# Convolution sums kept in PSUM, low parts of weights made on GpSimd, first tap on ScalarE

## The chip, the cores and the metric

One NeuronCore of a Trainium2 chip runs the whole kernel. The metric is the device time of one execution in microseconds (us). The engines are named as the profile names them: PE is TensorE (matmuls; PEld its weight loads), DVE is VectorE, ACT is ScalarE, POOL is GpSimd and SP is SyncE, which here only issues DMAs.

## The reference, cut to what matters

Two model blocks are computed for 512 latent tokens and 256 context tokens of width 1024. The first block has two layers; each layer projects the normalised input by one wide matrix and feeds a convolution module, a gated linear attention (GLA) with four heads that runs in both directions, and a softmax attention. The second block is not touched by the change. The convolution module is what the change is about:

```python
CONV_WIDTH = 31
def conv_module(val, glu, gate, dw_w, dw_b, ln_g, ln_b, w_o):
    u = val * jax.nn.sigmoid(glu)
    pad = CONV_WIDTH // 2
    u = lax.conv_general_dilated(u, dw_w[:, None, :], window_strides=(1,),
                                 padding=[(pad, pad)],
                                 dimension_numbers=('NWC', 'WIO', 'NWC'),
                                 feature_group_count=D_CONV) + dw_b
    u = jax.nn.silu(layer_norm(u, ln_g, ln_b)) * jax.nn.silu(gate)
    return u @ w_o
```

So each of the 512 channels is convolved over time with its own 31 weights. The GLA keeps a state per head, in chunks of 64 tokens: `S_t = diag(a_t) S_{t-1} + k_t^T v_t`, `o_t = q_t S_t`.

## The kernel before, in words

**Projections.** Activations lie transposed: channels on the 128 partitions, tokens along the free axis. Float32 precision is made from two fp32r parts: a matrix `w` is split into a high part `wh` and a low part `wl = w - wh`, the activations likewise into `hh` and `hl`. A projection of 1024 inputs onto 128 outputs loads one weight tile `wr` (128x1024) by DMA, ACT makes `wh` (line 283), DVE makes `wl` (line 284), and PE runs three matmuls per block of 128 inputs (`hh` by `wh`, `hl` by `wh`, `hh` by `wl`; all record line 315) into a PSUM tile `pp`. Three of the eight PSUM banks belong to `pp`, the other five in this stage to the pool `glaps`, whose tiles are called `pm`. ACT or DVE evacuates `pp`.

**The stage around the change.** In `_first_block`, for each layer, several generators are written into each other by `_weave`, and the tile scheduler then sets the order on each engine by the order of writing and by readiness. The first `_weave` joins on its main side `conv_in` (eight projections; ACT makes two 128x768 tiles `tf` of a pair, lines 791 and 794, and DVE multiplies them to the convolution input `u`, line 796), `conv_gate` (four projections, lines 818 to 820), `gla_in` (the low-rank projection, whose weights DVE splits in line 904, then queries and keys, lines 930 and 931, and values, line 917), and the first steps of the heads. Its other side is `conv_mix` and then `conv_norm`. The second `_weave` joins the four GLA heads with `merge`, the product of the convolution output and its merge gate.

**`conv_mix`.** For each of four chunks of 128 channels, DVE runs 31 taps over a row of 783 columns (512 latent tokens, 15 zeros, 256 context tokens; 512 in layer 1). The first tap (line 806) writes the chunk's slice of the SBUF tile `ca`, and each of the other thirty (line 809) multiplies a shifted `u` by a per-channel weight (in `sm`) and adds `ca`. The four slices are independent of one another, so the scheduler may mix two chunks. There are 2 x 4 x 30 = 240 taps of line 809.

**`conv_norm`.** It sums the chunks (lines 829, 832), takes mean and variance by matmuls (lines 620, 630), normalises, gates and splits the result into `bh` (ACT, line 867) and `bl` (DVE, line 871). The product with `w_conv_out` follows.

**A GLA head.** `gla_gate` has the gate matmuls (line 943), their evacuation by ACT (lines 944, 945), exponential and logarithm (946, 947, the latter with a table load), a sum on DVE (948), two scans (951, 953), the last columns (957, 958), the decay on ACT (960), products with keys and queries (962 to 973) and a transpose on PE (979). `gla_body` has the state contributions (PE, line 993), the chain of 22 state updates `SP` on DVE (line 1003), which read the contributions from PSUM, the attention pairs (PE, line 1014; DVE, line 1016), the output (lines 1024 and 1028) and its norm. Each of these matmul groups takes one `pm` bank and holds it until the engine that reads it is done.

The functions that the change touches, with the line numbers of the profile:

Of the kernel before, what the change touches and what calls it, by code (L numbers as in the profile page):

```python
# [9 lines left out]
F32 = mybir.dt.float32  # L10
# [4 lines left out]
AF = mybir.ActivationFunctionType  # L15
ALU = mybir.AluOpType
AX = mybir.AxisListType
PSUM = bass.MemoryType.PSUM

P = 128  # L20
# [6 lines left out]
TAPS = 31  # L27
# [230 lines left out]
class _K:  # L258
# [12 lines left out]
    def split(self, spec, spare=None):  # L271

        nk, nc_ = spec[3], spec[5]
        n = nk * nc_
        r = self.raw(spec)[:, :n]
        if spare is None:
            hi = self.wh.tile([P, 1024], F32R, tag="wh", name="wh")[:, :n]
            lo = self.wh.tile([P, 1024], F32R, tag="wl", name="wl")[:, :n]
        else:
            c = slice(TX + P * spare, TX + P * spare + n // KT)  # L280
            hi, lo = self.hh[:, :, c], self.hl[:, :, c]
            r = r.rearrange("p (k c) -> p k c", k=KT)
        self.nc.scalar.activation(hi, r, AF.Copy)  # L283
        self.nc.vector.tensor_tensor(out=lo, in0=r, in1=hi.bitcast(F32), op=ALU.subtract)  # L284
        return hi, lo

    @staticmethod
# [266 lines left out]
def _weave(main, fill, n_main, n_fill, drain=True):  # L554

    acc = 0.0
    for _ in main:
        acc += n_fill / n_main
        while acc >= 1.0:
            acc -= 1.0  # L560
            next(fill, None)
    if drain:
        for _ in fill:
            pass


def _chain(*gens):
    for g in gens:
        yield from g


def _first_block(K, ctx, resp):
    tc, nc, a = K.tc, K.nc, K.a
    V, S, G, T = nc.vector, nc.scalar, nc.gpsimd, nc.tensor
# [8 lines left out]
    def layer(l, res, t3p, ctx2, pend):  # L583
# [21 lines left out]
        def vec(name, i=0, p0=0, p1=P, half=False):  # L605
            c = _S1[name] + i - (h0 if half else g0)
            return (smh if half else sm)[p0:p1, c:c + 1]
# [172 lines left out]
        AL = TX + 15 + TC if need else TX  # L780
# [3 lines left out]
        ca = big.tile([P, 4, AL], F32, tag="A", name="ca")  # L784
# [14 lines left out]

        def conv_mix():  # L800
            for c in range(4):
                for t0 in range(0, TAPS, 4):
                    for t in range(t0, min(t0 + 4, TAPS)):
                        x, w = u[:, c, t:t + AL], vec("cw", c * TAPS + t)
                        if t == 0:
                            V.tensor_scalar(out=ca[:, c, :], in0=x, scalar1=w, scalar2=vec("dwb", c), op0=ALU.mult,
                                            op1=ALU.add)
                        else:
                            V.scalar_tensor_tensor(out=ca[:, c, :], in0=x, scalar=w, in1=ca[:, c, :], op0=ALU.mult,  # L809
                                                   op1=ALU.add)  # L810
                    yield

        def conv_gate(gt):
# [59 lines left out]
            yield  # L873


        with tc.tile_pool(name="gla", bufs=1) as gp, tc.tile_pool(name="glaps", bufs=8 - K.pp_banks, space=PSUM) as pm:
            masks = gp.tile([P, 2, P], U8, name="masks")
            mf = t3(256)
            nc.scalar.dma_start(out=mf.rearrange("p (a b) -> p a b", a=2), in_=a["masks"])
# [162 lines left out]
            AT = [gp.tile([P, 512], F32, name=f"at{d}") for d in range(2)]  # L1042
            for t_ in AT:
                G.memset(t_, 0.0)
            cin, cb = conv_in(), []
            next(cin)
            next(cin)
# [4 lines left out]
            def gla_():  # L1052

                yield from gla_gate(0)
                for hd in range(4):
# [7 lines left out]
            gla = gla_()  # L1063
            n_gla, n0 = (43, 3) if need else (27, 3)
            n_tap = 37 if need else 34
            _weave(_chain(cin, conv_gate(gt), gla_in(), itertools.islice(gla, n0)),
                   _chain(pend(t3, pm_) if pend else (), conv_mix(), conv_norm(gt, cb, pm_)), 15 + n0, n_tap)
            _weave(gla, merge(lambda: cb, "w_conv_out", 0, True), n_gla - n0, 28 if need else 16)


# [702 lines left out]
```

## Time and profile before

| quantity | value |
|---|---|
| runs | 2756.91, 2754.63, 2762.05 us; median 2756.91 |
| profiled execution | 2754.25 us, span 2752.4 us, mean granted PE clock 0.978 |
| PE busy | 2622.0 us (95% of the span), 15260 instructions |
| DVE busy | 1980.2 us (72%), 3689 instructions |
| ACT busy | 1087.8 us (40%), 1812 instructions |
| POOL busy | 27.4 us (1%), 93 instructions |
| chain that ended last, by engine | PE 79%, DVE 15%, ACT 3%, DMA 2%, issue 2% |
| in it, by line | PE line 315 64%, DVE taps (line 809) 4%, DVE low parts (284) 2%, DVE state updates (1003) 2% |

The span is the profiled execution from its first to its last instruction; the execution's own time is 1.85 us longer. Busy times are sums over the whole span, so they average over stages with different limits; the stages that matter here lie at 60 to 300 us (layer 0) and 940 to 1220 us (layer 1). The chain is followed back from the last instruction to what released each step.

### The profile page before, as it was taken

What the parts mean: (1) busy time and instruction counts of PE and PEld (TensorE: products, weight loads), DVE (VectorE), ACT (ScalarE), POOL (GpSimd) and SP (SyncE); (2) the same over time, 40 slices, a digit from 0 to 9 for tenths busy, and PEclk for the clock granted to TensorE, in tenths of its full rate; (3) what the DMA queues carried; (4) which work ended last, traced back from release to release, by engine and by line L of the source; (5) the groups of instructions that cost most, each with busy time, mean ns of one, the idle gap of its engine ahead of it and who ended that gap; (6) DMA issues with size and microseconds to landing.
All of it is one profiled execution on the core that took longest, in us unless ns stands there. A gap on an engine that the chain in (4) does not pass through costs nothing.

```text
span 2752.4 us, 38523 instructions
## 1 busy us (share of the span) xinstructions
PE 2622.0 (95%) x15260; PEld 2265.3 (82%) x15260; DVE 1980.2 (72%) x3689; ACT 1087.8 (40%) x1812; POOL 27.4 (1%) x93
## 2 busy tenths in 40 slices
PE   5998899999899999699999999999999999999998
PEld 3887778888788788578878888888888988888887
DVE  5998565677875599766888588775776786645655
ACT  3234423354532333534545345442333444422332
POOL 0000000000000000000000000000000000000000
PEclk9998999999999999899999999999999999999999
DMA  6210103112253232023134333344432332222322
GB/s 210 64 57 29 39 28 103 51 34 62 68 153 104 84 96 67 25 69 110 53 118 142 119 119 114 113 128 126 138 101 77 86 89 82 77 77 85 92 69 77
DMA packets 78116, 243.27 MB, mean 88 GB/s; under 512 B 9968, under 2 KB 16496, under 8 KB 77808
## 3 DMA queue, kind: packets, MB, share of 16 engines
q1 hardware_dynamic: 72448, 233.37, 27.7%
q10 hardware_dynamic: 5488, 7.44, 0.9%
q8 instruction: 120, 1.97, 0.3%
q14 instruction: 60, 0.49, 0.1%
HBM read 238.68 MB, written 2.10 MB: 87 GB/s over the span
## 4 chain that ended last, share of the span: by engine, by line
PE 79%; DVE 15%; ACT 3%; DMA 2%; issue 2%; ACTq 0%; DVEq 0%
PE pp L315 64%; PE pm L315 5%; DVE ca L809 4%; PE ov L1259 2%; DVE wl L284 2%; PE sc L1229 2%; DVE SP L1003 2%; PE tr L1249 2%; ACT wh L283 1%; PE pm L630 1%; PE pm L1028 1%; DMA m<-wpack 1%; PE pm L620 1%; PE pm L1652 1%; DVE t L953 1%
## 5 line engine op out<-in xcount | busy, mean ns | idle before, releaser
L315 PE MATMUL pp<-hh,wh 128*128 128x512 f32 (+1 forms) x2080 | 772.0, 373 | 31.9 <-ACT bk L931 13.2
L315 PE MATMUL pp<-hh,wl 128*128 128x512 f32 (+1 forms) x2080 | 767.5, 372 | 27.8 <-DVE wl L284 27.7
L315 PE MATMUL pp<-hl,wh 128*128 128x512 f32 (+1 forms) x2080 | 766.9, 371 | 1.0 <-DVE hl L467 0.9
L283 ACT ACTIVATE wh<-wr 128x1024 fp32r<-128x1024 f32 (+1 forms) x316 | 313.7, 994 | 701.3 <-PE pp L315 594.9
L284 DVE TENSOR_TENSOR wl<-wr,wh 128x1024 fp32r<-128x1024 f32 (+1 forms) x316 | 359.9, 1140 | 182.9 <-ACT wh L283 178.0
L315 PEld LDWEIGHTS pp<-hh,wh 128*128 128x128 f32 x2080 | 396.1, 191 | 99.3 <-ACT bk L931 13.8
L315 PEld LDWEIGHTS pp<-hh,wl 128*128 128x128 f32 x2080 | 395.6, 191 | 99.4 <-DVE wl L284 34.5
L315 PEld LDWEIGHTS pp<-hl,wh 128*128 128x128 f32 x2080 | 396.4, 191 | 65.7 <-DVE hl L467 3.5
L809 DVE SCALAR_TENSOR_TENSOR ca<-u,sm,ca 128x783 f32<-128x783 f32 (+1 forms) x240 | 201.6, 887 | 1.1
L315 PE MATMUL pp<-hh 128*128 128x256 f32 x544 | 155.3, 285 | 1.7 <-DVE vl L1559 1.7
L315 PE MATMUL pp<-hl,hh 128*128 128x256 f32 x544 | 155.1, 285 | 1.6 <-DVE hl L284 1.6
L315 PE MATMUL pp<-hh,hl 128*128 128x256 f32 x544 | 154.9, 285 | 0.0
L414 DVE CUSTOM_DVE_ANT_0 junk<-mw,cond,bmod 128x1024 bf16<-128x1024 f32 x104 | 132.7, 1276 | 2.8 <-DMA mw<-modw 2.5
L315 PE MATMUL pp<-wl,hh 128*128 128x256 f32 x448 | 127.7, 286 | 0.6 <-DVE wl L284 0.4
L315 PE MATMUL pp<-wh,hl 128*128 128x256 f32 x448 | 126.6, 284 | 0.0
L315 PE MATMUL pp<-wh,hh 128*128 128x256 f32 x448 | 125.8, 284 | 0.8 <-ACT tf L735 0.8
L315 PE MATMUL pp<-bh,wh 128*128 128x512 f32 (+1 forms) x288 | 105.3, 367 | 4.6 <-DVE merged L770 2.3
L315 PEld LDWEIGHTS pp<-hh 128*128 128x128 f32 x544 | 105.5, 194 | 4.0 <-issue 2.5
L315 PEld LDWEIGHTS pp<-hl,hh 128*128 128x128 f32 x544 | 105.5, 194 | 2.5 <-DVE hl L284 1.9
L315 PEld LDWEIGHTS pp<-hh,hl 128*128 128x128 f32 x544 | 105.4, 194 | 0.0
L315 PE MATMUL pp<-bl,wh 128*128 128x512 f32 (+1 forms) x288 | 103.3, 360 | 0.0
L315 PE MATMUL pp<-bh,wl 128*128 128x512 f32 (+1 forms) x288 | 103.0, 360 | 0.0
(371 smaller groups left out, 4833.2 us busy)
## 6 DMA issues: line engine op xcount, KB each, us to landing
wr<-wpack SPq DMA_DIRECT2D x308, 512.0 KB, 3.7
mw<-modw SPq DMA_DIRECT2D x80, 512.0 KB, 3.8
wr<-wpack SPq DMA_DIRECT2D x48, 256.0 KB, 2.6
m<-wpack SPq DMA_DIRECT2D x16, 512.0 KB, 8.4
cond<-cond ACTq DMA_DIRECT2D x5, 512.0 KB, 4.5
res<-xT SPq DMA_DIRECT2D x4, 512.0 KB, 4.8
tf<-xT SPq DMA_DIRECT2D x8, 256.0 KB, 2.8
out<-t SPq DMA_DIRECT2D x16, 128.0 KB, 1.8
```

Of the source, the lines that this page charges most:

```text
L283: self.nc.scalar.activation(hi, r, AF.Copy)
L284: self.nc.vector.tensor_tensor(out=lo, in0=r, in1=hi.bitcast(F32), op=ALU.subtract)
L315: mm(o, lhsT=lhs[a], rhs=r[b], start=first and p == 0, stop=last and p == 2)
L414: pin(V.tensor_tensor_reduce(out=junk, in0=w, in1=self.cond[:, v, :], scale=1.0, scalar=bias[:, j:j + 1], op0=ALU.mult, op1=ALU.add, accum ...
L620: T.matmul(p1[:, i:i + 1], lhsT=x[:, o:o + P], rhs=ones[:, 0:1], start=True, stop=True)
L630: T.matmul(p2[:, o:o + P], lhsT=r[:, i:i + 1].to_broadcast([P, P]), rhs=ident, start=True, stop=True)
L809: V.scalar_tensor_tensor(out=ca[:, c, :], in0=x, scalar=w, in1=ca[:, c, :], op0=ALU.mult, op1=ALU.add)
L953: V.tensor_tensor_scan(out=cum[64:128, ::-1], data0=reset[64:128, ::-1], data1=ls[64:128, ::-1], initial=0.0, op0=ALU.mult, op1=ALU.add)
L1003: V.scalar_tensor_tensor(out=SP[r, n_, :], in0=SP[r, c_, :], scalar=dec[r, c_:c_ + 1], in1=con[c_][r, :], op0=ALU.mult, op1=ALU.add)
L1229: T.matmul(sc[:, s - k0:e - k0], lhsT=qT[:, t * P:t * P + P], rhs=kT[pi][:, s:e], start=pi == 0, stop=pi == 1)
L1249: T.transpose(tr[:, jj * 256 + q * P:jj * 256 + q * P + P], pr[q][:, (j + jj) * P:(j + jj + 1) * P], ident)
L1259: T.matmul(ov, lhsT=vhl[:, kts[j0 + jj], g].rearrange("p a b -> p (a b)"), rhs=x_[:, jj * 256:jj * 256 + 256], start=j0 + jj + pi == 0, st ...
```

## The change

It has four parts. (1) The sum of a chunk is kept in a PSUM tile `acc` (called `pc`, 128x1024 float32, two banks, one buffer); each tap reads and writes it there, and the last tap writes the result to `ca`. (2) The first tap is an ACT activation with scale and bias into `acc`. (3) Between the start of `conv_in` and the end of the first `_weave` of each layer, the low part of a weight tile is made by POOL; the split of line 904 stays on DVE, and so do the low parts of the second `_weave`. (4) The pool `glaps` has three banks instead of five.

```diff
         self.nc.scalar.activation(hi, r, AF.Copy)
-        self.nc.vector.tensor_tensor(out=lo, in0=r, in1=hi.bitcast(F32), op=ALU.subtract)
+        E = self.nc.gpsimd if self.pool_lo else self.nc.vector
+        E.tensor_tensor(out=lo, in0=r, in1=hi.bitcast(F32), op=ALU.subtract)
         return hi, lo
...
             for c in range(4):
+                acc = pc.tile([P, 1024], F32, tag="pc", name="pc")[:, :AL]
                 for t0 in range(0, TAPS, 4):
                     for t in range(t0, min(t0 + 4, TAPS)):
                         x, w = u[:, c, t:t + AL], vec("cw", c * TAPS + t)
                         if t == 0:
-                            V.tensor_scalar(out=ca[:, c, :], in0=x, scalar1=w, scalar2=vec("dwb", c), op0=ALU.mult,
-                                            op1=ALU.add)
+                            S.activation(acc, x, AF.Identity, scale=w, bias=vec("dwb", c))
                         else:
-                            V.scalar_tensor_tensor(out=ca[:, c, :], in0=x, scalar=w, in1=ca[:, c, :], op0=ALU.mult,
-                                                   op1=ALU.add)
+                            V.scalar_tensor_tensor(out=acc if t < TAPS - 1 else ca[:, c, :], in0=x, scalar=w, in1=acc,
+                                                   op0=ALU.mult, op1=ALU.add)
                     yield
...
-        with tc.tile_pool(name="gla", bufs=1) as gp, tc.tile_pool(name="glaps", bufs=8 - K.pp_banks, space=PSUM) as pm:
+        with tc.tile_pool(name="gla", bufs=1) as gp, tc.tile_pool(name="glaps", bufs=3, space=PSUM) as pm, \
+                tc.tile_pool(name="convps", bufs=1, space=PSUM) as pc:
...
+            K.pool_lo = True
             cin, cb = conv_in(), []
...
+            K.pool_lo = False
             _weave(gla, merge(lambda: cb, "w_conv_out", 0, True), n_gla - n0, 28 if need else 16)
```

Lines shift: 284 becomes 285, 806 becomes 808, 809 becomes 810, the other lines of the stage move on by one (to 800) or two.

The order on the engines moves with it. On DVE, at the end of the first chunk of layer 0, stand before (`u` is the convolution input, `wl` a low part):

```order
L809 SCALAR_TENSOR_TENSOR ca<-u,sm,ca 128x783
L284 TENSOR_TENSOR wl<-wr,wh 128x1024
L809 SCALAR_TENSOR_TENSOR ca<-u,sm,ca 128x783
L806 TENSOR_SCALAR ca<-u,sm 128x783
L809 SCALAR_TENSOR_TENSOR ca<-u,sm,ca 128x783 x5
L284 TENSOR_TENSOR wl<-wr,wh 128x1024
L809 SCALAR_TENSOR_TENSOR ca<-u,sm,ca 128x783 x5
```

and now, with the last tap of the first chunk in the fifth row and the second chunk behind it:

```order
L810 SCALAR_TENSOR_TENSOR pc<-u,sm,pc 128x783 x12
L797 SCALAR_TENSOR_TENSOR u<-tf 128x512
L810 SCALAR_TENSOR_TENSOR pc<-u,sm,pc 128x783 x3
L797 SCALAR_TENSOR_TENSOR u<-tf 128x256
L810 SCALAR_TENSOR_TENSOR pc<-u,sm,pc 128x783
L810 SCALAR_TENSOR_TENSOR ca<-u,sm,pc 128x783
L810 SCALAR_TENSOR_TENSOR pc<-u,sm,pc 128x783 x8
```

The second chunk's first tap stood on DVE among taps of the first chunk; now the taps of one chunk stand in a row, with no low part between them.

On ACT, ahead of the second head of layer 0, stand before (`bk` are keys evacuated from `pp`, `dec` is the decay, which reads what DVE wrote to `last`):

```order
L283 ACTIVATE wh<-wr 128x1024
L960 ACT_TABLE_LOAD
L960 ACTIVATE dec<-last 128x12
L966 ACTIVATE t_2019<-t_2008 128x768
L964 ACTIVATE t_2016<-t_2016 128x768
L970 ACTIVATE t_2008<-t_2008 128x768
L930 ACTIVATE bk<-pp,sm 64x256
L931 ACTIVATE bk<-pp,sm 64x256
```

and now:

```order
L283 ACTIVATE wh<-wr 128x1024
L932 ACTIVATE bk<-pp,sm 64x256
L933 ACTIVATE bk<-pp,sm 64x256
L932 ACTIVATE bk<-pp,sm 64x256
L933 ACTIVATE bk<-pp,sm 64x256
L962 ACT_TABLE_LOAD
L962 ACTIVATE dec<-last 128x12
```

The four key evacuations of 256 columns moved ahead of the decay and its table load.

On PE, at the state contributions (`gv`, `kn`) and attention pairs (`bq`, `kin`) of the first head of layer 0, stand before:

```order
L315 MATMUL pp<-hl,wh 128x512
L993 MATMUL pm<-gv,kn 128x128 x4
L1014 MATMUL pm<-bq,kin 128x128 x4
L315 MATMUL pp<-hh,wl 128x512
L315 MATMUL pp<-hh,wh 128x512
```

and now:

```order
L995 MATMUL pm<-gv,kn 128x128 x4
L945 MATMUL pm<-lr,wup 128x512
L945 MATMUL pm<-lr,wup 128x256
L995 MATMUL pm<-gv,kn 128x128 x8
L1016 MATMUL pm<-bq,kin 128x128 x2
L316 MATMUL pp<-hh,wh 128x256
```

The four attention matmuls in one piece are split into twos, with projection matmuls between, and the gate matmuls of the next head (line 945 now) stand directly ahead of the second group of contributions.

## Rows read from the trace of the kernel before

**Rows 1.** Windows: us, then PE, PEld, DVE, ACT, POOL busy; clock; DMA.
```profile
80.00:100.00 20.00, 20.00 (x115) 17.62 (x114) 19.82 (x22) 4.62 (x7) 0.00 (x0) 1.00 0.23 68
...
260.00:280.00 20.00, 7.86 (x47) 6.66 (x45) 19.35 (x33) 13.97 (x20) 0.00 (x0) 0.71 0.01 1
```

**Rows 2.** Waits of PE, 60 to 290 us: total us, times, longest us.
```profile
PE pp L315 <- ACT bk L931: 13.2, 2, 8.1
PE pp L909 <- DVE wh L904: 4.7, 1, 4.7
```

**Rows 3.** Waits of PE, 940 to 1160 us, the largest.
```profile
PE pp L315 <- DVE wl L284: 10.4, 2, 8.9
```

**Rows 4.** Groups of DVE by form, 60 to 230 us: busy us, mean ns, idle.
```profile
L809 DVE SCALAR_TENSOR_TENSOR ca<-u,sm,ca 128x783 f32<-128x783 f32 x120 | 118.1, 1031 | 0.7
L284 DVE TENSOR_TENSOR wl<-wr,wh 128x1024 fp32r<-128x1024 f32 x17 | 20.7, 1220 | 3.0 <-ACT wh L283 3.0
...
L806 DVE TENSOR_SCALAR ca<-u,sm 128x783 f32<-128x783 f32 x4 | 2.7, 684 | 0.1
...
L796 DVE SCALAR_TENSOR_TENSOR u<-tf 128x256 f32<-128x256 f32 x4 | 1.7, 422 | 0.1
```

**Rows 5.** Timeline of DVE, both layers: start us, us together, instruction, count.
```profile
72.43 6.38 DVE L809 SCALAR_TENSOR_TENSOR ca<-u,sm,ca 128x783 f32<-128x783 f32 x6
...
96.39 1.22 DVE L284 TENSOR_TENSOR wl<-wr,wh 128x1024 fp32r<-128x1024 f32 x1
97.52 4.81 DVE L809 SCALAR_TENSOR_TENSOR ca<-u,sm,ca 128x783 f32<-128x783 f32 x5
...
969.61 3.89 DVE L809 SCALAR_TENSOR_TENSOR ca<-u,sm,ca 128x512 f32<-128x512 f32 x5
...
1056.49 4.06 DVE L809 SCALAR_TENSOR_TENSOR ca<-u,sm,ca 128x512 f32<-128x512 f32 x6
```

**Rows 6.** Groups of DVE by form, 940 to 1100 us.
```profile
L809 DVE SCALAR_TENSOR_TENSOR ca<-u,sm,ca 128x512 f32<-128x512 f32 x120 | 83.4, 744 | 0.4
...
L464 DVE SCALAR_TENSOR_TENSOR t<-res,gsc,nps 128x512 f32<-128x512 f32 x8 | 5.5, 738 | 0.0
```

**Rows 7.** Timeline of ACT, 258 to 285 us.
```profile
258.75 1.02 ACT L864 ACTIVATE cd<-cd,sm 128x768 f32<-128x768 f32 x1
...
276.18 0.21 ACT L960 ACTIVATE dec<-last 128x12 f32<-128x12 f32 x1 [0.96 <-DVE last L958]
...
279.10 0.47 ACT L930 ACTIVATE bk<-pp,sm 64x256 f32<-64x256 f32 x1
```

**Rows 8.** Timeline of PE, 255 to 285 us.
```profile
261.09 0.37 PE L1014 MATMUL pm<-bq,kin 64*128 64x128 f32 x1
...
281.07 0.80 PE L315 MATMUL pp<-hh,wh 128*128 128x512 f32 x1 [8.13 <-ACT bk L931]
```

**Rows 9.** Timeline of DVE, the twelve state updates of the first head.
```profile
267.24 4.49 DVE L1003 SCALAR_TENSOR_TENSOR SP<-SP,dec,pm 64x128 f32<-64x128 f32 x12
```

**Rows 10.** Timelines of DVE and of POOL, 940 to 941 us.
```profile
940.18 0.16 DVE L305 SCALAR_TENSOR_TENSOR t<-t,nv 128x4 f32<-128x4 f32 x1
940.61 1.09 DVE L891 TENSOR_SCALAR nbz<-sm 128x4 f32<-128x4 f32 x1 [0.27 <-PE pp L315]
...
940.64 0.74 POOL L882 MEMSET reset<- 128x768 bf16 x1 [888.35 <-PE pp L315]
```

**Rows 11.** Groups of POOL by form, whole run.
```profile
L1593 POOL TENSOR_SCALAR_AFFINE_SELECT t<-t 128x128 f32<-128x128 f32 x32 | 15.9, 498 | 89.8 <-ACT t L1590 89.8
...
L1044 POOL MEMSET at<- 128x512 f32 x4 | 2.0, 530 | 0.1
```

**Rows 12.** Timeline of DVE, state updates of a later head, layer 1.
```profile
1147.42 6.39 DVE L1003 SCALAR_TENSOR_TENSOR SP<-SP,dec,pm 64x128 f32<-64x128 f32 x17
```

**Rows 13.** Timelines of ACT and PE: a high part and its first matmul.
```profile
85.62 1.06 ACT L283 ACTIVATE wh<-wr 128x1024 fp32r<-128x1024 f32 x1 [2.00 <-PE pp L315]
...
93.88 0.40 PE L315 MATMUL pp<-hh,wh 128*128 128x512 f32 x1
```

## The prediction

> **What bounds the kernel now.** I read the busy time by stretches first. In layer 0's conv stage TensorE (PE) is busy 20.00 us of 20 while VectorE (DVE) is busy 19.82 of 20; in 260 to 280 us, at the hand-over to the GLA heads, PE does 7.86 of 20, with a granted clock of 0.71 [rows 1]. So through the conv taps both engines are full, and what DVE is late with is paid afterwards, in the stretch 220 to 285 us. The waits of PE name the holes: 4.7 us once for the low-rank weights that DVE splits in line 904, and 13.2 us in two pieces for the evacuation of keys by ScalarE (ACT), line 931 [rows 2]. In layer 1 the one large entry is 10.4 us for a low part of weights (line 284) that stands on DVE behind the scans [rows 3]. These 28 us are about all that the two stages have to give; the projections themselves are dense.
>
> **Low parts to GpSimd (POOL).** The 17 low parts of a layer cost DVE 1.220 us each [rows 4], and the next instruction starts 1.13 us after one (96.39 to 97.52) [rows 5]. Between the first and last tap of layer 0 DVE now has 14 of them, in the new order 2, because two of the merge come forward: 12 x 1.13 = -13.6 us of DVE. In layer 1 I count 14 fewer: -15.8 us. On POOL no such operation is in the trace. Its 128x512 memset takes 530 ns and its 128x128 select 498 ns [rows 11]: by the memset a 1024-wide one takes 1.0 us, by the select scaled with its columns up to 4.0. I take 2. It matters little, since what hides it is lead: the high part of one block is made at 85.62 + 1.06 us and its first matmul starts at 93.88 [rows 13], 7.2 us later, more than the upper end, and a projection comes only every 8 us. If that lead were gone, PE would wait by the difference, 0 to 3 us per projection.
>
> **First tap to ACT.** DVE loses four operations of 0.684 us [rows 4], about 0.6 us of issue each: -2.4 us, in layer 1 -1.8. ACT gains four; its nearest row, a scale-and-bias over 128x768, took 1.02 us [rows 7]. There is one accumulator. So the first tap of chunks 2 to 4 can start only when DVE has finished the chunk before, and the new DVE order puts the next taps directly behind. At each of three boundaries DVE stands still for about 1.02 us: +3 us, in layer 1 (two thirds as wide) +2.4. ACT waits in its queue meanwhile, with the evacuation of the next projection behind it. The banks of the projection's own pool cover that while it is under some 8 us.
>
> **Taps into PSUM.** This is the dearest unknown. Six taps of one chunk in a row took 6.38 us, (6.38 - 1.03) / 5 = 1.07 us from tap to tap; five that change between chunks took 4.81, (4.81 - 1.03) / 4 = 0.945 [rows 5]. The tap itself lasts 1.031 us [rows 4]. The difference is the wait for one's own result. Before, the scheduler mixes two chunks, and I count 18 neighbouring pairs of the same chunk in layer 0; with one accumulator 94 are neighbours. With spacings as in SBUF that is 76 x 0.125 = +9.5 us. In layer 1 the same two spacings are (3.89 - 0.75) / 4 = 0.785 and (4.06 - 0.75) / 5 = 0.66 [rows 5], 83 more pairs: +10.2 us. What writing PSUM costs no row shows. Reading it costs nothing: with one operand there, line 464 takes 738 ns, the tap of the same 512 columns all in SBUF 744 [rows 6]. I take 1.07 for the new spacing, nearest to that row. My bounds are 0.945, as if the wait vanished, and 1.20, as if the write took once more the same 0.125. The Trainium skill, "Perfetto Trace Analysis", section "Optimizing Scalar/DVE Operations", speaks against this edit: it charges a DVE instruction about 125 ns of access on PSUM against 60 on SBUF, which by an estimate from that page would add 0.065 us to each of 240 taps, 15.6 us of DVE. The rows on reading do not agree with it; no run here shows writing.
>
> **POOL against DVE.** A small DVE instruction that takes 0.16 us took 1.09 beside a 0.74 us memset on POOL [rows 10]: the two engines can block each other. By the Trainium skill, "SBUF — State Buffer", section "Who interferes with whom", a DVE instruction with two SBUF inputs contends with a POOL instruction that reads SBUF, one with a single SBUF input does not; so the taps would run free and the old form would not have. That no run here shows. I charge the operations other than taps: eight gate products (0.42 us for the 256-wide form, [rows 4]) and four merges come some 0.5 us after the high part is made, just when POOL works. With 1 to 2 us of standstill for three or four of them: +4.5 us in layer 0, +3 in layer 1. The lower bound is 0.
>
> DVE's sum to the last tap is -13.6 - 2.4 + 3 + 9.5 + 4.5 = +1.0 us in layer 0 and -15.8 - 1.8 + 2.4 + 10.2 + 3 = -2.0 in layer 1. **The freed DVE time is nearly all spent again.**
>
> **What PE gets.** Line 904 now stands behind 62 taps on DVE instead of 74 and behind no low part, over 12 us earlier, so its 4.7 us [rows 2] go. The 13.2 us [rows 2] go as well. The second stretch starts at 281.07 behind a 8.13 us wait [rows 8]: the key evacuations (279.10) stood on ACT behind the decay (276.18), which waits for DVE [rows 7]. In the new ACT order they stand ahead of it. But a new wait takes that place. GLA has three banks instead of five, and the first attention pair (261.09 now, [rows 8]) needs a bank that the chain of twelve state updates frees: it starts at 267.24 and lasts 4.49 us [rows 9], so to 271.7, a wait of about 10 us in place of 13.2. Layer 0 up to the first head: -4.7 - 3.2 + 1.0 = -6.9. Each of the three later heads waits for banks; by the state updates of a head (6.39 us for 17, 0.375 each [rows 12]) a bank comes three or so updates late: +1.1 us each, +3.3. Layer 0: -3.6 us. Layer 1: the late low part stands one step (about 1.5 us) earlier on DVE, conv ends 2 us earlier but PE is nearly full there (take -1), and three heads give back 1.1 each: -1.5 - 1 + 3.3 = +0.8. Nothing else in the program changes.
>
> **Sum.** -3.6 + 0.8 = -2.8 us against the profiled execution's 2754.25: 2751.5. That execution lies 2.66 us below the median of the runs shown, 2756.91; I put the forecast at **2752**. Some 0.3% (8.3 us, to 2748.6 or 2765.2) is what a measurement here can tell from no change.
>
> **Rivals.**
> 1. *Writing PSUM hides the chain* (spacing 0.945 in layer 0, 0.66 in layer 1). Conv ends 9.5 and 10 us earlier, and with little contention 14 and 13 us. Then the heads start earlier and PE's holes [rows 1 to 3] close: by at most 10 us in layer 0 and 8 in layer 1 beyond the sum, 2752 - 18 = 2734; half of it is 2743. For it: DVE is full there [rows 1], so each freed microsecond counts. Against: the wait for a result exists wherever the result lies.
> 2. *Slower: writing PSUM lengthens it.* Place: the 94 pairs of each layer. Each 0.01 us costs 0.94 us per layer; from 1.15 on, conv ends 7.5 us later in each layer, and as the norm, the merge and the heads hang on it, PE waits for nearly all: 1.15 gives 2752 + 15 = 2767, the bound of 1.20 gives 2776. It decides from about 1.145.
> 3. *Three banks starve the heads.* If each head waited for its whole chain (6.4 us [rows 12]) less the 1.1 counted, three heads in layer 1 alone lose 16 us: 2768. Against: the new PE order puts projections between the pairs.
> 4. *POOL blocks the taps*, 2 us of standstill for each of 34 low parts, not for some small operations alone: +68 - 7.5 = 60 us of DVE that PE waits for, some 2810. For it: [rows 10]; against: the operations of that row are others.
> 5. *No effect*: PE is the bound wherever the taps run, DVE's time is free. 2754 to 2757, inside my forecast.
>
> **Chances.** Forecast with rival 5: 0.45 (own range 2745 to 2762, of which 0.09 under 2748.6). Rival 1: 0.26, rival 2: 0.13, rival 3: 0.08, rival 4: 0.08. Faster by over 0.3%: 0.26 + 0.09 = 0.35; slower: 0.13 + 0.08 + 0.08 = 0.29; the rest 0.36. The range 2735 to 2773 leaves out rival 4 (0.08), the far half of rival 2 (0.06) and the far end of rival 1 (0.06).
>
> **What would show it.** Right: taps of 128x783 in PSUM 1.07 us apart; three DVE holes of about 1 us ahead of the second, third and fourth chunk, released by line 808; the 4.7 us wait gone; PE waiting some 10 us for a bank ahead of the first attention pair, where the wait for line 931 stood; POOL's low parts 1 to 3 us with no PE wait on them. Wrong: a spacing under 1.0 or over 1.14; taps of 2 us and more beside POOL; PE waits of over 3 us per head in the later heads.

## The result, and the profile after

The changed kernel takes 2779.01 us (median of 4 runs, 2777.62 to 2780.0) against 2757.05 us (4 runs, 2754.63 to 2762.05) of the kernel before on the same chip: a ratio of 1.0078, 95% interval 1.0066 to 1.009. It is 22 us slower. The forecast was 2752, the range ended at 2773.

The page of the changed kernel: the chain that ended last by line, and of the costliest groups the one of POOL (busy us, mean ns, idle before, releaser):

```profile
PE pp L316 66%; PE pm L316 5%; PE ov L1263 2%; PE sc L1233 2%; PE tr L1253 2%; DVE SP L1005 1%; DVE wl L285 1%; POOL wl L285 1%; PE pm L631 1%; PE pm L1030 1%; DMA m<-wpack 1%; ACT wh L283 1%; DMA wr<-wpack 1%; PE pm L1656 1%; PE pm L621 0%
...
L285 POOL TENSOR_TENSOR wl<-wr,wh 128x1024 fp32r<-128x1024 f32 x34 | 81.4, 2398 | 933.9 <-DVE nv L449 744.1
```

A low part takes POOL 2.40 us (the forecast took 2). The taps, 4% of the chain before, are no longer among its lines: most of the chain is PE's, 82% where it had 79%.

The groups of DVE by form, 60 to 230 us, answer to [rows 4]. Two of them, the values `gv` and the products `merged`, are not among those rows; before, they were:

```profile
L917 DVE TENSOR_TENSOR gv<-pp,t 128x512 f32<-128x512 f32 x6 | 4.1, 685 | 0.0
L820 DVE SCALAR_TENSOR_TENSOR merged<-tf 128x768 f32<-128x768 f32 x4 | 3.8, 955 | 0.0
```

and now:

```profile
L810 DVE SCALAR_TENSOR_TENSOR pc<-u,sm,pc 128x783 f32<-128x783 f32 x116 | 120.3, 1037 | 7.7 <-ACT pc L808 4.4
L797 DVE SCALAR_TENSOR_TENSOR u<-tf 128x256 f32<-128x256 f32 x4 | 5.4, 1360 | 5.0 <-ACT tf L795 5.0
L821 DVE SCALAR_TENSOR_TENSOR merged<-tf 128x768 f32<-128x768 f32 x4 | 4.5, 1137 | 0.0
...
L919 DVE TENSOR_TENSOR gv<-pp,t 128x512 f32<-128x512 f32 x6 | 4.1, 690 | 4.3 <-PE pp L316 4.3
```

and its timeline to [rows 5]:

```profile
72.23 11.78 DVE L810 SCALAR_TENSOR_TENSOR pc<-u,sm,pc 128x783 f32<-128x783 f32 x11 [1.14 <-ACT pc L808]
...
108.23 8.55 DVE L810 SCALAR_TENSOR_TENSOR pc<-u,sm,pc 128x783 f32<-128x783 f32 x8 [1.08 <-ACT pc L808]
```

Taps in PSUM come (11.78 - 1.03) / 10 = 1.075 us apart, and the hole at a chunk boundary is 1.08 us.

The waits of PE, 60 to 300 us, answer to [rows 2]:

```profile
PE pm L945 <- DVE SP L1005: 7.2, 1, 7.2
PE pp L316 <- ACT bk L933: 5.9, 2, 3.8
PE pp L316 <- POOL wl L285: 3.2, 4, 1.5
```

**Where the 22 us are.** The same instruction can be followed through both traces. The four splits of the convolution output in layer 1 (first row of each pair) and the third of the four splits of the heads' output `go` there (second row) are on DVE, before:

```profile
1116.01 2.48 DVE L871 TENSOR_TENSOR bl<-merged,bh 128x512 fp32r<-128x512 f32 x4
...
1294.66 0.68 DVE L745 TENSOR_TENSOR bl<-go,bh 128x512 fp32r<-128x512 f32 x1
```

and after:

```profile
1126.06 2.48 DVE L872 TENSOR_TENSOR bl<-merged,bh 128x512 fp32r<-128x512 f32 x4
...
1317.18 0.68 DVE L746 TENSOR_TENSOR bl<-go,bh 128x512 fp32r<-128x512 f32 x1
```

The first come 10.05 us later, the second 22.52. Read in the same way at five places, by the ends of the instructions, the kernels of this study stand against the kernel before as follows (one profiled execution each, us; A is the first sum of the chunks in layer 0, B the first split of `go` behind layer 0's heads, C the second convolution input of layer 1, D and E the two rows above):

| kernel | A | B | C | D | E | time, median |
|---|---|---|---|---|---|---|
| changed | +4.5 | +3.5 | +10.6 | +10.0 | +22.5 | 2779.0 |
| e1: three banks | -2.2 | +3.6 | +2.3 | +2.3 | +16.1 | 2771.1 |
| e2: GpSimd alone | +24.6 | +23.0 | +32.6 | +61.5 | +72.6 | 2826.4 |
| e3: PSUM sums, no GpSimd | +3.7 | +13.9 | +12.6 | +32.6 | +41.9 | 2795.9 |
| e4: banks given back | +6.2 | +1.6 | +9.3 | +8.9 | +20.3 | 2767.0 |
| e5: late GpSimd | +4.8 | +3.9 | +4.7 | +5.7 | +19.6 | 2775.4 |
| e6: e4 and e5 | +5.3 | +0.3 | +1.3 | +3.8 | +16.6 | 2774.6 |
| e7: e6, two sums | +3.6 | +1.5 | +2.6 | +2.7 | +6.6 | 2759.6 |
| e8: four banks | -0.7 | -1.1 | -3.0 | -3.0 | +7.4 | 2764.9 |
| e9: before, GpSimd in the heads | +1.5 | -1.4 | -2.4 | +10.3 | +35.3 | 2783.7 |
| e10: e9, first tap on ScalarE | +1.6 | -7.2 | -8.7 | -3.2 | +5.4 | 2760.6 |
| e11: before, first tap on ScalarE | -1.4 | -2.8 | -4.9 | -3.3 | +0.7 | 2751.1 |
| e12: e7, GpSimd in the heads | +4.4 | +0.3 | +0.5 | +8.3 | +22.5 | 2778.9 |
| e13: changed, filler | +4.2 | +3.2 | +10.5 | +9.9 | +12.1 | 2769.3 |
| e14: e11, filler | -2.6 | -4.1 | -6.2 | -4.6 | +0.9 | 2756.6 |
| e15: e7, filler | +5.8 | +0.5 | +1.7 | +1.9 | +5.1 | 2757.6 |

So the changed kernel loses 3.5 us in layer 0, some 7 at the start of layer 1 (B to C), nothing in its conv stage (C to D) and 12.5 in its heads (D to E). A single execution scatters by some microseconds: the profiled one of e13 took 2763.8 us and that of e8 2758.9, both some 6 us below their medians, those of e4 (2772.8) and e9 (2789.7) some 6 us above. The verdicts below rest on the medians, the places on the traces.

**The start of layer 1.** The norm of the layer's input is a chain of small DVE instructions and then splits (`hl`). DVE of the changed kernel:

```profile
941.12 3.39 DVE L302 TENSOR_SCALAR g<-g 128x4 int32<-128x4 int32 x1
...
945.92 2.21 DVE L305 TENSOR_TENSOR t<-y 128x4 f32<-128x4 f32 x1
...
968.82 4.67 DVE L468 SCALAR_TENSOR_TENSOR hl<-t,mod,hh 128x256 fp32r<-128x256 f32 x4
```

beside POOL:

```profile
941.00 2.40 POOL L285 TENSOR_TENSOR wl<-wr,wh 128x1024 fp32r<-128x1024 f32 x1 [744.10 <-DVE nv L449]
943.35 0.74 POOL L884 MEMSET reset<- 128x768 bf16 x1
...
945.78 2.34 POOL L285 TENSOR_TENSOR wl<-wr,wh 128x1024 fp32r<-128x1024 f32 x1
...
967.52 4.89 POOL L285 TENSOR_TENSOR wl<-wr,wh 128x1024 fp32r<-128x1024 f32 x2 [19.41 <-ACT wh L283]
```

Instructions of 0.16 to 0.17 us last 3.39 and 2.21 us. The second ends with POOL's low part (948.1 us); the first outlasts one (943.4) and ends at 944.5, among short memsets of POOL. Four splits, 0.42 us apart when nothing holds them, take 4.67 us together.

### The profile page after: what moved, and what is told of

It reads as the page before. It is cut to its first block, busy times and chain, and to the rows that moved or that the text cites. A ratio compares the mean times of both kernels' runs of the same rounds, so it can differ in the third digit from the quotient of the medians.

```text
span 2775.9 us, 38521 instructions
## 1 busy us (share of the span) xinstructions
PE 2641.7 (95%) x15260; PEld 2279.1 (82%) x15260; DVE 1972.0 (71%) x3647; ACT 1094.3 (39%) x1820; POOL 108.0 (4%) x127
## 4 chain that ended last, share of the span: by engine, by line
PE 82%; DVE 9%; issue 3%; ACT 3%; DMA 2%; POOL 1%; SPq 0%; ACTq 0%; POOLq 0%; DVEq 0%
PE pp L316 66%; PE pm L316 5%; PE ov L1263 2%; PE sc L1233 2%; PE tr L1253 2%; DVE SP L1005 1%; DVE wl L285 1%; POOL wl L285 1%; PE pm L631 1%; PE pm L1030 1%; DMA m<-wpack 1%; ACT wh L283 1%; DMA wr<-wpack 1%; PE pm L1656 1%; PE pm L621 0%
## 5 line engine op out<-in xcount | busy, mean ns | idle before, releaser
L285 DVE TENSOR_TENSOR wl<-wr,wh 128x1024 fp32r<-128x1024 f32 (+1 forms) x282 | 318.8, 1131 | 171.9 <-ACT wh L283 164.7
L810 DVE SCALAR_TENSOR_TENSOR pc<-u,sm,pc 128x783 f32<-128x783 f32 (+1 forms) x232 | 207.8, 896 | 13.1 <-ACT pc L808 6.3
L285 POOL TENSOR_TENSOR wl<-wr,wh 128x1024 fp32r<-128x1024 f32 x34 | 81.4, 2398 | 933.9 <-DVE nv L449 744.1
```

Of the source, the lines that this page charges most:

```text
L285: E.tensor_tensor(out=lo, in0=r, in1=hi.bitcast(F32), op=ALU.subtract)
L810: V.scalar_tensor_tensor(out=acc if t < TAPS - 1 else ca[:, c, :], in0=x, scalar=w, in1=acc, op0=ALU.mult, op1=ALU.add)
```

## The experiments

The runs of the kernel before that go with them have medians of 2754.5 us (e1 to e4), 2756.3 (e5 to e8), 2755.8 (e9 to e12) and 2756.8 (e13 to e15); for the changed kernel it was 2757.1. So two times of different groups can be 2 to 3 us nearer or farther than they look, and the ratios are the better measure there. "Lower parts" in the edits is line 284 (285 after the change).

**e1, three banks alone.** Edit to the kernel before:

```diff
-tc.tile_pool(name="glaps", bufs=8 - K.pp_banks, space=PSUM) as pm:
+tc.tile_pool(name="glaps", bufs=3, space=PSUM) as pm:
```

> The kernel before with three banks for GLA instead of five, nothing else. Theory A (the banks cost most of the loss): the four heads of layer 1, from the low part of the convolution output (1118.5 us before) to the last gated output, lose about 12 us as in the changed kernel, and layer 0 some 3; 2757 + 12 to 15, so 2769 to 2772. Rival B (the loss in the heads comes from the order that the other parts bring, not from the banks): within 3 us of 2757.

Measured: 2771.14 us, ratio 1.0057 (1.0042 to 1.0072). Theory A holds: up to D it is 2 us behind, at E 16. The state updates of a head show how the banks do it. Before, the 22 of the last head run in one piece on DVE (start, us together, count, idle before and its releaser):

```profile
1212.56 8.29 DVE L1003 SCALAR_TENSOR_TENSOR SP<-SP,dec,pm 64x128 f32<-64x128 f32 x22
```

With three banks the contributions they read are written in pieces, as banks come free, and DVE waits for PE:

```profile
1221.43 0.34 DVE L1003 SCALAR_TENSOR_TENSOR SP<-SP,dec,pm 64x128 f32<-64x128 f32 x1 [0.40 <-PE pm L993]
...
1224.12 2.62 DVE L1003 SCALAR_TENSOR_TENSOR SP<-SP,dec,pm 64x128 f32<-64x128 f32 x7 [1.69 <-PE pm L993]
...
1228.08 4.89 DVE L1003 SCALAR_TENSOR_TENSOR SP<-SP,dec,pm 64x128 f32<-64x128 f32 x13 [0.37 <-PE pm L993]
```

The chain takes 11.5 us (1221.43 to 1232.97) instead of 8.3, 3.2 more in this head. That accounts for a part of the 13.8 us between D and E; PE's own waits for state updates are short there (1110 to 1320 us: total, times, longest):

```profile
PE pm L1014 <- DVE SP L1003: 2.5, 4, 0.8
```

**e2, GpSimd alone**, with sums in SBUF and five banks. Edit to the kernel before:

```diff
-        self.nc.vector.tensor_tensor(out=lo, in0=r, in1=hi.bitcast(F32), op=ALU.subtract)
+        E = self.nc.gpsimd if self.pool_lo else self.nc.vector
+        E.tensor_tensor(out=lo, in0=r, in1=hi.bitcast(F32), op=ALU.subtract)
...
+            K.pool_lo = True
             cin, cb = conv_in(), []
```

> The kernel before with only the low parts on GpSimd in the conv stage; sums stay in SBUF, five banks. Taps then have two SBUF inputs. Theory A (GpSimd and a VectorE instruction with two SBUF inputs block each other): each of 34 low parts of about 2.4 us stops VectorE for up to 2.4 us, minus 28 x 1.13 us that VectorE saves: conv ends 10 to 20 us later per layer, 2757 + 20 to 40. Rival B (only particular instructions are blocked): taps keep 0.945 and 1.07 us spacing and VectorE gains 14 us per layer; 2740 to 2757.

Measured: 2826.36 us, ratio 1.0265 (1.0239 to 1.0291). Theory A holds, with more than it allowed: +24.6 us at A. By form, 60 to 240 us:

```profile
L810 DVE SCALAR_TENSOR_TENSOR ca<-u,sm,ca 128x783 f32<-128x783 f32 x120 | 141.9, 1231 | 1.0
L807 DVE TENSOR_SCALAR ca<-u,sm 128x783 f32<-128x783 f32 x4 | 6.8, 1702 | 0.1
```

A tap with both operands in SBUF costs 1.231 us in the mean instead of 1.031 [rows 4], so 120 x 0.2 = 24 us; the tap with its sum in PSUM, beside the same work of POOL, costs 1.037. That is the difference that the Trainium skill, "SBUF — State Buffer", section "Who interferes with whom", makes between two SBUF inputs and one, and here the runs show it. The first tap (line 807) has one SBUF input beside its scalars and was held all the same, 1.702 us instead of 0.684; the section excepts instructions that enter a two-port mode and names `tensor_scalar` among those that can.

That the 24 us of the taps equal A (+24.6) is a coincidence: the 14 low parts that left DVE give back 16 us up to A, and longer first taps (4 us), longer products `u` (2) and 10 us more of standing still take them again. In layer 1, between C and D, DVE stands still for 30 us instead of 4, for 16 of them waiting for the values' projections (line 918); theory A's sum has no such term, and why these projections are late was not followed.

**e3, sums in PSUM without GpSimd.** Edit to the changed kernel:

```diff
-            K.pool_lo = True
```

> The changed kernel with all low parts on VectorE again: sums in PSUM, first tap on ScalarE, three banks. Theory A (GpSimd's share of the loss is the 7 us at the start of layer 1, where it blocks the norm and the splits): that start is as before (u of the first chunk at about 963 us plus the shift of layer 0), but VectorE carries 12 to 14 low parts more in each conv stage, so conv ends 12 us later in layer 0 and PE waits: about 2785. Rival B (low parts on GpSimd only cost, because VectorE's time is free): 2770 or less.

Measured: 2795.89 us, ratio 1.0145 (1.0129 to 1.016). Neither number was right: GpSimd is worth 17 us to the changed kernel (2795.9 against 2779.0; 19 when each is set against its own runs of before), not 6. The place that theory A named holds: from B to C this kernel loses nothing (+13.9, +12.6) where both kernels with GpSimd there lose 7 and 10. Against e1, which has the same three banks, the sum in PSUM with ScalarE's first tap costs 2795.9 - 2771.1 = 24.8 us as long as VectorE makes all low parts. What VectorE or PE waits for in these 24.8 us was not followed.

**e4, banks given back** to GLA once the first weave is written. Edit to the changed kernel:

```diff
             K.pool_lo = False
+            late.close()
+            more.append(late.enter_context(tc.tile_pool(name="glaps2", bufs=2, space=PSUM)))
```

> The changed kernel, but the two banks of the sum go back to GLA when the first weave of the layer has been written (heads 2 to 4 have five banks again). Theory A (banks cost the 12 us in layer 1's heads): most of it returns, 2779 - 8 to 12, so 2767 to 2771, and PE waits for a bank on state updates (7.6 us and 7.2 us in the changed kernel) shrink to under 5 in all. Rival B: within 3 us of 2779.

Measured: 2767.00 us (5 runs, 2766.26 to 2775.19), ratio 1.0049 (1.0032 to 1.0065); by the medians 12 us of the 22 return, against its own runs of before 9 (12.5 us over instead of 22), as theory A has it. But its five runs spread over 9 us (three near 2766.7, two at 2773 and 2775), and in the profiled one, of 2772.8 us, layer 1's heads are hardly shorter (11.4 us over before instead of 12.5). So the return is shown in the total and not in its place. Waiting was not all of it.

**e5, GpSimd later in layer 1.** Edit to the changed kernel (`need` is true in layer 0):

```diff
-            K.pool_lo = True
...
             for c in range(4):
+                K.pool_lo = need or c > 1
                 th, vb = tf(), tf()
```

> The changed kernel, but in layer 1 GpSimd makes low parts only from the third chunk's projections on, after the norm of the layer's input and its splits are through; layer 0 as changed. Theory A (GpSimd blocks the norm and the splits at the start of layer 1, 7 to 8 us): the second convolution input of layer 1 comes 8 us earlier against layer 0's end, and the time falls from 2779 to 2771 to 2773. Rival B (the wait moves on, PE has the same work left in the heads): conv ends earlier, the heads do not, 2777 to 2780.

Measured: 2775.43 us (2769.52 to 2780.51), ratio 1.0062 (1.0044 to 1.008). Between the two: the start of layer 1 gets 6 us back (C at +4.7 instead of +10.6), the heads lose 14 instead of 12.5, and 3.6 of the 6 remain in the medians. The intervals of the two ratios overlap (the changed kernel's is 1.0066 to 1.009), so the gain in the total is not told from none; the one at C is read from the traces.

**e6, both repairs** (e4 and e5).

> Late GpSimd in layer 1 (as in the run before) and the two banks given back to GLA after the first weave (as in the run of that edit, 2767). Theory A (the two losses add): 2767 - 7 = 2760, some 0.2% above the kernel before. Rival B: the granted clock and the deferred work in layer 1's heads take part of it back, 2765 to 2768.

Measured: 2774.59 us (2768.59 to 2777.82), ratio 1.0057 (1.0039 to 1.0076). Theory A fails by 15 us, and B, which has the direction, by 7. At D the kernel is only 3.8 us behind, at E 16.6: the 6 us gained ahead of the heads are kept, but the heads lose 12.9, as in the changed kernel (12.5), although they have five banks again. Against e4 the intervals overlap: the two repairs do not add, but e6 is not shown to be slower than e4 either, nor, by its interval, faster than the changed kernel.

**e7, two sums in layer 1**, where 512 columns fit one bank. Edit to e6:

```diff
-acc = pc.tile([P, 1024], F32, tag="pc", name="pc")[:, :AL]
+acc = pc.tile([P, 1024 if need else 512], F32, tag="pc", name="pc")[:, :AL]
...
-tc.tile_pool(name="convps", bufs=1, space=PSUM)
+tc.tile_pool(name="convps", bufs=1 if need else 2, space=PSUM)
```

> As the run with both repairs, and in layer 1, where a sum is 512 columns and fits one bank, two sums of one bank instead of one of two, so that two chunks can be mixed. Theory A (the wait for one's own result costs VectorE 83 x 0.12 = 10 us there): neighbouring taps 0.66 us apart instead of 0.785 in part of the pairs, the third boundary without a hole, conv of layer 1 ends 5 to 10 us earlier; but PE is full there, so the time falls by 2 to 5 us against the run with both repairs. Rival B: no change, as PE bounds the stage.

Measured: 2759.55 us (10 runs, 2755.88 to 2763.09), ratio 1.0007 (0.9997 to 1.0017): 15 us under e6, level with the kernel before. Theory A had the direction and not the place. The convolution output comes only 1 us earlier (D); the gain lies in the heads, which lose 3.9 us instead of 12.9. The taps do come closer where two chunks mix, 14 of them in 9.30 us, (9.30 - 0.75) / 13 = 0.66 us apart, but the end of the convolution hardly moves by it.

**e8, four banks** in the kernel before (`bufs=4`).

> The kernel before with four banks for GLA (five before; three cost 16.7 us of 2754.5 by themselves). Theory A (each bank taken away makes a group of a head wait for the reader of an earlier one): four cost between a third and a half of three, +5 to +8 us. Rival B (a particular group needs the third and fourth bank at once, as the pairs of attention do with the contributions): four cost nothing, within 2 us of before.

Measured: 2764.89 us (10 runs), ratio 1.0024 (1.0015 to 1.0034). Near theory A: half of what three banks cost by the medians (8.6 of 16.7 us), 0.4 of it by the ratios, all of it behind D.

**e9 to e12, towards a better version.** e9 sets the switch for GpSimd around the second weave alone in the kernel before; e10 adds the first tap on ScalarE, e11 is that tap alone, e12 adds the switch of e9 to e7. The first tap:

```diff
-                            V.tensor_scalar(out=ca[:, c, :], in0=x, scalar1=w, scalar2=vec("dwb", c), op0=ALU.mult,
-                                            op1=ALU.add)
+                            S.activation(ca[:, c, :], x, AF.Identity, scale=w, bias=vec("dwb", c))
```

> The kernel before, sums in SBUF and five banks, with GpSimd making the low parts only in the second weave (heads and merge), where PE of the kernel before waits 20.6 us in layer 1 for low parts that stand on VectorE behind scans. Most VectorE operations there (state updates, gated output, merge sums) read one operand from PSUM. Theory A (these are not blocked, and the low part no longer stands behind the scans): the waits of 8.9 and 9.7 us fall to those of the chain behind them, PE's clock falls less often, 2755 - 5 to 15: 2740 to 2750. Rival B (GpSimd blocks the scans and the products with two SBUF operands, 2.4 us each time, and the heads hang on VectorE's chain): 2755 to 2775.

> As the run with GpSimd in the second weave, and the first tap of each chunk on ScalarE into the chunk's own SBUF slice. Theory A (four operations of 0.6 us leave VectorE where it is full, and with four slices no chunk waits for another): 1 to 4 us under that run. Rival B (ScalarE's queue delays an evacuation by its wait, or the order changes): 0 to 5 us over it.

> The kernel before with only the first tap on ScalarE, into the chunk's own slice of SBUF. Theory A: as there is no single accumulator, no hole before a chunk; VectorE's conv stretch ends 2 us earlier in each layer; 2751 to 2756, nothing that a measurement can tell. Rival B: 2757 to 2762, since the order of the stage changes with it.

> The run with two sums in layer 1 and both repairs (2759.6), and GpSimd in the second weave as well. Theory A (what GpSimd gives in the heads adds to it): as far under 2759.6 as the run with GpSimd in the second weave alone is under the kernel before. Rival B (the heads there have other waits by now): within 3 us of 2759.6.

Measured: e9 2783.7 us (ratio 1.0092, 1.0068 to 1.0116), e10 2760.61 (1.0018, 1.0008 to 1.0027), e11 2751.13 (0.999, 0.9976 to 1.0005), e12 2778.87 (1.0082, 1.0065 to 1.0098). GpSimd in the heads harms: e9 lies above the ranges of both theories, in B's direction, e12 lies 19 us above e7 where theory B had at most 3, and e11 is where its theory A had it. In layer 0 of e9 the scans and splits are held (1754 and 951 ns before):

```profile
L954 DVE TENSOR_TENSOR_SCAN t<-reset,t 64x768 f32<-64x768 bf16 x3 | 7.2, 2409 | 0.1
L872 DVE TENSOR_TENSOR bl<-merged,bh 128x768 fp32r<-128x768 f32 x4 | 5.7, 1486 | 0.0
```

The low parts indeed no longer hold PE, but in layer 1 the keys that hang on the held chain do:

```profile
PE pm L980 <- DVE bk L974: 22.9, 4, 7.6
```

That e10 lies 23 us under e9, where its edit was expected to account for 4, is resolved by place only: of the 30 us between the two profiled executions, 6 are gained in layer 0 (B), 7 between C and D and 16 between D and E. e11 is the best kernel of the study by its median, 4.6 us under the kernel before, which the interval does not tell from no change.

**e13 to e15, filler matmuls.** In layer 1 the heads of all these kernels differed more than their waits. Two rows of the changed kernel suggest why (PE, layer 1; the first row stands 3.4 us behind the end of a 4.9 us wait for a bank, the second right behind a wait for a low part):

```profile
1138.39 0.63 PE L316 MATMUL pp<-hl,wh 128*128 128x512 f32 x1
1143.90 0.79 PE L316 MATMUL pp<-hh,wl 128*128 128x512 f32 x1 [4.89 <-DVE wl L285]
```

These take 0.63 us where the same matmul takes 0.39: the granted clock has fallen to half (1.2 instead of 2.4 GHz). Adding up PE's busy time in the stretches of half clock between D and E gives 14.8 us before, 28.5 in the changed kernel. So e13 puts work that changes no result into the waits:

```diff
                     tr = pm_()
+                    if p0 == 4 and not need and hd:
+                        for _ in range(16):
+                            T.matmul(tr, lhsT=h[0][0][:, 0:P], rhs=h[0][0][:, 0:512], start=True, stop=True)
```

> The changed kernel with 16 matmuls of 512 columns more ahead of the key transposes of heads 2 to 4 in layer 1; their result is overwritten by the transposes. At full clock they take 16 x 0.22 = 3.5 us each time, 10.6 us in all, and they stand where PE of the changed kernel waits 4 to 7 us for low parts or banks. Theory A (a large part of what the heads lose is PE at its lower clock after those waits: 28.5 us of busy time at half clock there against 14.8 before): the clock falls later or for less, the heads stage is 3 to 8 us shorter in spite of the added work, 2771 to 2776. Rival B (the waits themselves set the time, the clock follows): no change where the fillers fit into the waits, up to +10 us where they don't, 2779 to 2789.

> The kernel before with the first tap on ScalarE (2751.1 us) and the same 48 added matmuls in layer 1. Theory A: PE was 17.6 us busy at half clock in that stage, which costs 8.8 us; half of it comes back, 2745 to 2750. Rival B: 2751 to 2760.

> The run with two sums in layer 1 and both repairs (2759.6 us, 26.0 us busy at half clock in the heads of layer 1), with the same 48 added matmuls. Theory A: 3 to 8 us under it, 2752 to 2757. Rival B: 2759 to 2769.

Measured: e13 2769.33 us (2763.79 to 2771.36), ratio 1.0042 (1.0026 to 1.0059), 9.7 us under the changed kernel with 48 matmuls more. At D the two are level to 0.2 us, at E e13 is 10.4 us ahead. PE of e13 at the same place:

```profile
1136.77 5.57 PE L982 MATMUL pm<-hh 128*128 128x512 f32 x16
...
1142.63 0.39 PE L316 MATMUL pp<-hh,wh 128*128 128x512 f32 x1
1143.76 0.50 PE L316 MATMUL pp<-hh,wl 128*128 128x512 f32 x1 [0.74 <-DVE wl L285]
```

The low part comes at 1143.8 as before, so the wait was not shortened, only filled; but what follows runs at full clock. The stage between D and E as a window (us, span, busy PE, PEld, DVE, ACT, POOL, mean clock, DMA), of the kernel before, the changed one and e13:

```profile
1118.50:1295.30 176.80, 147.45 (x876) 124.12 (x875) 124.94 (x288) 70.31 (x102) 0.00 (x0) 0.91 0.22 69
```

```profile
1128.50:1317.90 189.40, 163.14 (x902) 136.55 (x903) 126.85 (x290) 73.44 (x106) 0.00 (x0) 0.89 0.22 66
```

```profile
1128.40:1307.50 179.10, 164.78 (x950) 136.84 (x951) 127.13 (x289) 73.34 (x106) 0.00 (x0) 0.96 0.23 69
```

Busy time at half clock is 9.0 us in e13. Half of the 19.5 us that disappeared is 9.75, nearly the whole gain of 10.2 in the stage. In the two other kernels the fillers won nothing: e14 2756.64 us (ratio 1.0008, 0.9996 to 1.0019), 5 over e11, as rival B has it, and e15 2757.57 (1.0004, 0.9994 to 1.0015), 2 under e7, less than theory A wanted. In e15 there was nearly as much to win as in e13. The traces show what differs (from the end of D's splits to the end of E, us):

| kernel | stage | PE busy at half clock | PE idle |
|---|---|---|---|
| before | 176.8 | 14.8 | 29.3 |
| changed | 189.3 | 28.5 | 26.2 |
| e13: changed, filler | 179.1 | 9.0 | 14.4 |
| e11 | 180.9 | 17.6 | 30.8 |
| e14: e11, filler | 182.3 | 19.6 | 20.5 |
| e7 | 180.7 | 26.0 | 17.6 |
| e15: e7, filler | 180.1 | 24.6 | 10.0 |
| e6 | 189.7 | 44.6 | 23.6 |
| e4 | 188.3 | 42.2 | 24.6 |
| e1 | 190.6 | 24.9 | 29.6 |
| e9 | 201.9 | 62.7 | 29.0 |
| e10 | 185.5 | 32.4 | 23.2 |

The fillers took 8 to 12 us of idle time from PE in all three, but more than 2 us of half-clock time in e13 alone, and there alone the stage got shorter by more than 1 us. Half of the difference in half-clock time is also as much as the 9 us by which e7's heads are shorter than e6's, and 15 of the 16 us between e9 and e10. Why the fillers kept the clock up in one kernel and not in the others was not tried.

## Why the prediction was wrong, step by step

**Right.** The tap spacing in PSUM (1.07 forecast, 1.075 measured), so rivals 1 and 2 fall; the taps of 1.037 us beside POOL let rival 4 fall, which e2 shows to hold in part (24 us) where the sums stay in SBUF. The hole at a boundary (1.02, 1.08). POOL's low part (2 us, 2.40), and nearly that it comes in time: no wait of PE for it was expected, and there are 7.2 us in the whole run, in eight pieces of at most 1.5. The charge for blocked operations in layer 0: the 256-wide gate products and the merges now take 4 x (1.360 - 0.422) + 4 x (1.137 - 0.955) = 4.5 us more, the number of the forecast. The 4.7 us wait for line 904 is gone. The charge for the three later heads of layer 0 was about right too (+3.3; their outputs `go` come 0.3 us later than before in the first head and 3.1 in the fourth).

**"DVE's sum to the last tap is ... +1.0 us in layer 0"**: measured +4.45 (A). What I left out is that freed DVE time can stand still. The sum has no term for waits of DVE on PE; the values come 9 us earlier than before, but DVE is there earlier still and waits 4.3 us for their projections (line 919), where it did not wait at all (line 917). Layer 0 ended at +3.5 instead of -3.6, and the 7.1 us between the two were lost up to the first head: 3.5 are this term; some 3 are the keys, whose wait of 13.2 us did not become one of 10 for a bank but 5.9 for the keys and 7.2 for a bank, at line 945 and not at the pair behind it; the norm has longer waits of PE besides (3.1 us for `y`, 1.9 for a sum).

**"I charge the operations other than taps: eight gate products and four merges"**: this step failed in layer 1. Work of the norm, whose small instructions [rows 10] I had used to show that blocking exists, stands at the very place where GpSimd starts. It costs 7 us at C; e3, which loses nothing there without GpSimd, and e5, which starts it later, show that it is GpSimd's.

**"Each of the three later heads waits for banks ... +1.1 us each"**: this is the step that failed most. The forecast for layer 1's heads was +3.3 and they lost 12.5. Three banks alone, in the kernel before, cost 16.7 us (e1), 13.8 of them here, four 8.6 (e8), and giving two back returned 9 to 12 (e4). Rival 3, with 2768 for starved heads, named the right resource and, at 16 us in layer 1, nearly the size that e1 has; I gave it 0.08. Its mechanism, a wait of PE for the whole chain of updates in each head, is not what the trace shows: in the changed kernel PE's waits for it are, 1110 to 1320 us (total, times, longest):

```profile
PE pm L1016 <- DVE SP L1005: 6.5, 5, 4.9
```

Three chains would be 19 us. And between D and E PE is idle 26.2 us in all instead of 29.3: the heads are longer although PE stands still less. How a missing bank lengthens them is seen in e1 for one head (3.2 us) and is open for the rest.

**What no step had** is the price of a wait beyond its length. Behind the waits shown PE works at half clock, and in layer 1's heads this costs the changed kernel 28.5 / 2 = 14 us against 7 before; e13 took 10 us back with the low part no earlier. So of the 12.5 us in the heads, about 7 are more half-clock time than before. PE's other busy time grew by 8.8 us, of which some 5 are matmuls that PE had not done by D (902 in the stage instead of 876, an estimate at 0.2 us each), and its idle time fell by 3.1. That the banks act mainly through the clock is not shown: in e1 half-clock time makes 5 of the 13.8 us, and the profiled execution of e4, with the banks given back, has more of it (42.2 us) than the changed kernel.

**Where the expected gain of GpSimd went.** With sums in PSUM it is real: 17 to 19 us (e3). But the PSUM sums cost 24.8 us by e1 and e3, and three banks 16.7. The change pays 41 to gain 19, and the 22 us are what is left. This is one order of the steps; taken first, GpSimd costs 72 us (e2). Of the two edits in the 24.8 us, the first tap on ScalarE costs nothing by itself where each chunk has its own slice (e11). The prediction charged the taps' longer spacing against the low parts that leave DVE, 19.7 against 29.4 us; that the first can cost the program 25 and the second bring it only 17 to 19 was not in it.

**Open.** e6 has less than e4 to repair and is not faster (2774.6 and 2767.0, with runs of both spread over 9 us); e9 and e10 differ by 23 us for one edit, in the heads nearly all by half-clock time. That each edit moves the scheduler's order in the heads, and the clock magnifies it, is my reading and was not tested; nor was it tried which of the moves in e10 does it.

## What to carry to other kernels

Moving work off a full engine is worth what the engine behind it then does earlier: follow the freed time to the first wait, and add the buffers that the move takes from another stage as a cost there. GpSimd beside VectorE was cheap here for taps that read one operand from PSUM (1.037 us) and dear for those with both in SBUF (1.231); list every two-operand instruction in the stretch, the small ones of a norm too, before switching it on. And where TensorE waits, look at the granted clock behind the wait: the same stage was 10 us longer or shorter by it here. Filling a wait is worth nothing by itself (e14, e15): see in the trace whether the clock stayed up.

## What was not expected of the hardware

- Useless matmuls made the changed kernel 9.7 us faster (e13): 48 of them took busy time at half clock in the stage from 28.5 us to 9.0. The same 48 left it nearly as it was in two other kernels (17.6 to 19.6, 26.0 to 24.6) and won nothing there.
- A small `tensor_scalar` on integers (line 302, 128x4) took 3.39 us instead of 0.17 beside one low part and the memsets of POOL behind it, and the first tap, with one SBUF input, was held in e2 as well (1.702 us instead of 0.684).
- VectorE writing PSUM cost next to nothing: 1.037 us for a tap of 783 columns with its sum in PSUM, 1.031 in SBUF. The Trainium skill, "Perfetto Trace Analysis", section "Optimizing Scalar/DVE Operations", charges by its figures (about 125 ns of access on PSUM, 60 on SBUF) some 65 ns more; these rows do not bear that out.
